# Ordering the chunks of a feed-forward block whose second product uses seven block products

## The chip, the cores and the metric

The kernel runs on one core of a Trainium2 chip. The metric is the device time of one execution in microseconds (us); less is better. A core has TensorE (PE: matmuls, and PEld: loads of the stationary operand), VectorE (DVE), ScalarE (ACT), GpSimd (POOL) and SyncE (SP), which here only starts transfers from memory. Each engine works through its own list of instructions in order, and waits where one of them needs what another engine or a transfer has not yet delivered.

## The reference

A decoder layer on `x` of 256 rows by 1024 columns in float32: a normalisation, a wide input projection, two attention mixers that are merged, an output projection with a residual, and then a feed-forward block and a last normalisation. The change touches the feed-forward block alone:

```python
h2 = rmsnorm(x, norm2_g[layer])
u = jax.nn.relu(h2 @ w_ff1[layer])          # 1024 -> 4096
x = x + (u * u) @ w_ff2[layer]              # 4096 -> 1024
...
return rmsnorm(x, norm_f_g)
```

## The kernel before, in words

**Chunks.** All weights stream through the core as a list of chunks, `CHUNKS` (line 23), each 128 partitions by 2048 float32 columns (1 MB) at most. The work on one chunk on TensorE is called its slot, and slots follow each other in the order of the list. The feed-forward block begins at chunk `C_FF` = 28 with 16 chunks `ff1` (each gives 256 of the 4096 hidden columns) and 16 chunks `ff2` (each takes 256 of them to all 1024 outputs). ff2 number i needs the activations of ff1 number i. In this text a chunk is named by its kind and number, such as ff2 0.

**Three matmuls for one.** The float32 product is made of three matmuls of a faster type (float32r): each operand is split into a high part (ScalarE copies it into that type: `whi`, `sh`, `ah`) and a low part (VectorE subtracts the high part from the original: `wlo`, `sl`, `al`). `mm3` (line 219) issues high x high, high x low and low x high. So for a chunk an engine each has a conversion to do, `split` (line 103), before TensorE can start.

**Seven products for eight.** An ff2 chunk is, with its activations, a product of 2 x 2 blocks: two halves of the hidden columns, two halves of the rows, two halves of the output columns. Done plainly this is eight block products of 512 columns, 24 matmuls. For the first `NSEVEN` = 11 ff2 chunks the kernel uses a scheme with seven block products, 21 matmuls, which accumulate over the chunks in seven PSUM banks (`P["1"]` to `P["7"]`). It needs sums of weight blocks (`w_sums`: tile `wt`, three subtractions and an addition in three instructions) and of activation blocks (`act_sums`: tile `aq`, four small instructions), and more splitting: three weight blocks are used as they are (`w_singles`: `sh`, `sl`), four are sums (`w_parts`: `whi`, `wlo`), and seven activation blocks (`act_parts`: `ah`, `al`). `combine` (line 880) puts the seven banks together into the residual `x1` at the end of these chunks. The other five ff2 chunks are done plainly and accumulate in four banks (`ops`).

**Order.** Nothing reorders the program: each engine's list is the order in which the code issues. `at(pos, f, ...)` notes a step, and `run_slot` (line 202) issues a slot's matmuls with each step put in at its share `pos` of the slot. So a step at 0.5 of a slot stands in its engine's list after the steps of 0.3, but it runs when its engine gets there and its inputs are ready. `slot_events(c)` (line 920) notes in slot c the conversions of chunk c+2 or c+3 and the load of chunk c+5.

**Buffers.** The raw weights, `whi` and `wlo` have three buffers each; a load waits on SyncE until the last conversion that reads the buffer's old content is done. `sh`, `sl`, `wt` and `aq` have two, `ah` and `al` three. Hidden columns of an ff1 chunk are summed in one PSUM bank (`acc0` from ff1 2 on) and leave it by a ReLU on ScalarE (`ur`), then a square (`aq`): `squares` (line 796).

**Order of chunks before.** ff1 0, then ff1 1, ff2 0, ff1 2, ff2 1, and so on to ff1 11, ff2 10; then the ff1 chunks 12 to 15 alone, then the plain ff2 chunks 11 to 15. In ff1 1's slot TensorE also transposes the residual into rows (`x1_rows`). The last two ff2 chunks, 14 and 15, form one last slot ordered by output bank, so that each bank's final work (`final_a`, `final_b`) can begin while the next is summed.

## Time and profile before

| | |
|---|---|
| three runs, median (lowest to highest) | 390.91 us (389.94 to 391.99) |
| profiled execution, whole time | 391.41 us |
| its span, first to last instruction | 389.5 us |
| first matmul of ff1 0, from the span's start | 199.80 us |
| last stage of matmuls ends | 383.43 us |
| mean granted TensorE clock | 0.988 |

The span begins with the first instruction and ends with the last; all places below are in us from its start. The feed-forward block is its second half. A row of a timeline gives start and duration, the engine, the line, the operation, output and inputs by the program's names, the shape, and in brackets the engine's idle time just before, with what ended it. The name `o` stands for the four banks o0 to o3.

### The profile page before, as it was taken

The numbers are of one execution on the slowest core, as the hardware profiler recorded it, in microseconds if no ns is written. First come the engines' busy times: TensorE is split into PE (matmuls) and PEld (weight loads), VectorE is DVE, ScalarE is ACT, GpSimd is POOL, SyncE is SP. The second block draws the span as 40 slices with busy tenths as digits, with TensorE's granted clock in tenths as the row PEclk, the third lists the DMA queues.
The fourth block names the chain that finished last, engine by engine and source line by source line (L and its number), as shares of the span: only waits on it lengthen the run. The fifth ranks groups of instructions, "written<-read, shape, count | busy, mean of one in ns | idle before, by whom it ended". The sixth has DMA issues, their size and how long they took to land.

```text
span 389.5 us, 5979 instructions
## 1 busy us (share of the span) xinstructions
PE 373.1 (96%) x2407; PEld 324.4 (83%) x2407; DVE 305.5 (78%) x443; ACT 231.4 (59%) x368; POOL 3.8 (1%) x14
## 2 busy tenths in 40 slices
PE   7999999999999999999998799999999999889993
PEld 6997888878888788779998599999998888888783
DVE  4968677887876869666969968999999999922565
ACT  6884455766755747444457567776666668451712
POOL 1000000000000000000000000000000000000001
PEclk9999999999999999999999699999999999999998
DMA  7977435233533334530846633566655556554003
GB/s 248 406 264 270 165 106 203 108 115 118 202 109 109 134 151 151 213 108 18 316 155 218 215 108 121 204 217 215 217 193 186 174 207 217 213 178 146 0 2 109
DMA packets 11260, 66.31 MB, mean 170 GB/s; under 512 B 1248, under 2 KB 2784, under 8 KB 3936
## 3 DMA queue, kind: packets, MB, share of 16 engines
q1 hardware_dynamic: 10800, 65.14, 46.8%
q10 hardware_dynamic: 432, 0.79, 0.5%
q8 instruction: 19, 0.31, 0.3%
q14 instruction: 9, 0.07, 0.0%
HBM read 64.87 MB, written 1.05 MB: 169 GB/s over the span
## 4 chain that ended last, share of the span: by engine, by line
PE 82%; DVE 8%; ACT 4%; issue 2%; DMA 1%; SPq 1%; POOLq 0%; POOL 0%; DVEq 0%; ACTq 0%
PE acc L217 51%; PE o L217 11%; PE yb L217 5%; PE tp L217 4%; DVE wlo L114 3%; PE kvbacc L217 2%; ACT whi L112 2%; PE qacc L217 2%; PE Sa L217 1%; DMA raw<-in_kva_dram 1%; PE Sb L217 1%; PE Sa L482 1%; PE Sb L482 1%; PE tp L298 1%; DVE wlo L862 1%
## 5 line engine op out<-in xcount | busy, mean ns | idle before, releaser
L114 DVE TENSOR_TENSOR wlo<-raw,whi 128x1024 fp32r<-128x1024 f32 (+3 forms) x87 | 114.5, 1333 | 28.9 <-ACT whi L112 28.8
L112 ACT ACTIVATE whi<-raw 128x1024 fp32r<-128x1024 f32 (+2 forms) x106 | 99.7, 975 | 46.9 <-PE acc L217 33.3
L217 PE MATMUL acc<-h2h,whi 128*128 128x256 f32 x240 | 66.8, 278 | 3.0 <-ACT ur L804 3.0
L217 PE MATMUL acc<-h2h,wlo 128*128 128x256 f32 x240 | 66.5, 277 | 0.0
L217 PE MATMUL acc<-h2l,whi 128*128 128x256 f32 x240 | 66.5, 277 | 0.0
L217 PE MATMUL acc<-whi,hTh 128*128 128x512 f32 (+1 forms) x128 | 50.8, 397 | 0.8 <-ACT whi L112 0.6
L217 PE MATMUL acc<-wlo,hTh 128*128 128x512 f32 (+1 forms) x128 | 50.6, 395 | 0.4 <-DVE wlo L114 0.2
L217 PE MATMUL acc<-whi,hTl 128*128 128x512 f32 (+1 forms) x128 | 49.4, 386 | 0.0
L217 PEld LDWEIGHTS acc<-h2h,whi 128*128 128x128 f32 x240 | 45.1, 188 | 3.9 <-ACT ur L804 3.4
L217 PEld LDWEIGHTS acc<-h2l,whi 128*128 128x128 f32 x240 | 45.1, 188 | 0.5
L217 PEld LDWEIGHTS acc<-h2h,wlo 128*128 128x128 f32 x240 | 45.1, 188 | 0.0
L860 ACT ACTIVATE whi<-wt 128x2048 fp32r<-128x2048 f32 x11 | 21.1, 1920 | 24.7 <-DVE wt L845 24.7
L217 PEld LDWEIGHTS acc<-whi,hTh 128*128 128x128 f32 x128 | 24.2, 189 | 6.8 <-ACT whi L112 1.1
L217 PEld LDWEIGHTS acc<-wlo,hTh 128*128 128x128 f32 x128 | 24.1, 188 | 5.5 <-DVE wlo L114 1.6
L217 PEld LDWEIGHTS acc<-whi,hTl 128*128 128x128 f32 x128 | 24.1, 188 | 4.3
L862 DVE TENSOR_TENSOR wlo<-wt,whi 128x2048 fp32r<-128x2048 f32 x11 | 25.1, 2286 | 0.4 <-ACT whi L860 0.4
L820 ACT ACTIVATE ah<-aq 128x896 fp32r<-128x896 f32 (+1 forms) x16 | 13.6, 852 | 18.1 <-PE o L217 10.0
L822 DVE TENSOR_TENSOR al<-aq,ah 128x896 fp32r<-128x896 f32 (+1 forms) x16 | 15.4, 960 | 6.7 <-ACT ah L820 6.7
L853 DVE TENSOR_TENSOR sl<-raw,sh 128x1536 fp32r<-128x1536 f32 x11 | 19.3, 1752 | 0.0
L217 PE MATMUL o<-wlo,ah 128*128 128x512 f32 (+1 forms) x47 | 18.9, 402 | 0.0
L217 PE MATMUL o<-whi,al 128*128 128x512 f32 (+1 forms) x47 | 18.8, 400 | 0.0
L217 PE MATMUL o<-whi,ah 128*128 128x512 f32 (+1 forms) x47 | 18.8, 400 | 0.0
(280 smaller groups left out, 759.5 us busy)
## 6 DMA issues: line engine op xcount, KB each, us to landing
raw<-in_ff_dram SPq DMA_DIRECT2D x32, 1024.0 KB, 4.8
raw<-in_gm_dram SPq DMA_DIRECT2D x8, 1024.0 KB, 4.8
raw<-in_wout_dram SPq DMA_DIRECT2D x4, 1024.0 KB, 4.8
raw<-in_q_dram SPq DMA_DIRECT2D x2, 1024.0 KB, 5.5
raw<-in_qm_dram SPq DMA_DIRECT2D x2, 1024.0 KB, 7.6
raw<-in_km_dram SPq DMA_DIRECT2D x2, 1024.0 KB, 5.8
raw<-in_vm_dram SPq DMA_DIRECT2D x2, 1024.0 KB, 4.8
raw<-in_upn_dram SPq DMA_DIRECT2D x2, 1024.0 KB, 4.8
```

The costliest lines, as they stand in the source:

```text
L112: act.activation(hi[c][:, a:b], raw[c][:, a:b], AF.Copy)
L114: dve.tensor_tensor(lo[c][:, a:b], raw[c][:, a:b], hi[c][:, a:b].bitcast(F32), op=ALU.subtract)
L217: pe.matmul(o, l, r, start=start, stop=stop, skip_group_check=True)
L298: pe.transpose(tp[:, j * 256 + t * 128:j * 256 + t * 128 + 128], src[:, t, (2 * i + j) * 128:(2 * i + j + 1) * 128], ident)
L482: pe.transpose(S[x][:, j, c:c + 128], P[:, 2 * x + j, c:c + 128], ident)
L820: act.activation(A[i][1][:, 0:b - a], aq[:, a:b], AF.Copy)
L822: dve.tensor_tensor(A[i][2][:, 0:b - a], aq[:, a:b], A[i][1][:, 0:b - a].bitcast(F32), op=ALU.subtract)
L853: dve.tensor_tensor(singles[c][1], v, singles[c][0].bitcast(F32), op=ALU.subtract)
L860: act.activation(hi[c], v, AF.Copy)
L862: dve.tensor_tensor(lo[c], v, hi[c].bitcast(F32), op=ALU.subtract)
```

## The change

The list of chunks begins with three ff1 chunks; then ff2 and ff1 chunks come in turns until the ff1 chunks are used up (ff2 0, ff1 3, ff2 1, ... ff2 12, ff1 15), and ff2 13, 14 and 15 stand at the end. `NSEVEN` is 13, so all ff2 chunks that stand in turns use seven products and three are plain. The sums of weights and of activations of a chunk become one step, `sums`, in which an instruction of one kind stands between two of the other. The steps move within the slots: the sums and the high singles of an ff2 chunk are issued in the ff1 slot three chunks ahead, the rest of its conversions in the ff2 slot two chunks ahead, its activations' parts too. `ah` and `al` have two buffers for three. The combining stands in the slots of ff1 15 and ff2 13.

```diff
-NSEVEN = 11
+NSEVEN = 13
...
-    + [("ff1", 0, 2048)]
-    + [(s, i + (s == "ff1"), 2048) for i in range(NSEVEN) for s in ("ff1", "ff2")]
-    + [("ff1", i, 2048) for i in range(NSEVEN + 1, 16)]
+    + [("ff1", i, 2048) for i in range(3)]
+    + [(s, i + 3 * (s == "ff1"), 2048) for i in range(NSEVEN) for s in ("ff2", "ff1")]
     + [("ff2", i, 2048) for i in range(NSEVEN, 16)]
...
-    def act_sums(i):
-        aq = A[i][0]
-        if i < NSEVEN:
-            for o, x, y, op in ((4, 0, 2, ALU.add), (5, 1, 0, ALU.subtract),
-                                (6, 4, 1, ALU.subtract), (7, 3, 6, ALU.subtract)):
-                dve.tensor_tensor(aq[:, o], aq[:, x], aq[:, y], op=op)
...
-            A[i] += [FB["p"].tile([128, 7, 128], F32R, name=n, bufs=3) for n in ("ah", "al")]
+            A[i] += [FB["p"].tile([128, 7, 128], F32R, name=n, bufs=2) for n in ("ah", "al")]
...
-    def w_sums(c):
+    def sums(c):
...
+        aq = A[CHUNKS[c][1]][0]
+
+        def a_sum(o, x, y, op):
+            dve.tensor_tensor(aq[:, o], aq[:, x], aq[:, y], op=op)
+
         dve.tensor_tensor(T[:, 0:2], b[:, 1:4:2], b[:, 0, None, :].to_broadcast([128, 2, 512]),
                           op=ALU.subtract)
+        a_sum(4, 0, 2, ALU.add)
+        a_sum(5, 1, 0, ALU.subtract)
         dve.tensor_tensor(T[:, 2], b[:, 3], T[:, 0], op=ALU.add)
+        a_sum(6, 4, 1, ALU.subtract)
         dve.tensor_tensor(T[:, 3], b[:, 2], T[:, 2], op=ALU.subtract)
+        a_sum(7, 3, 6, ALU.subtract)
...
+        if seven(c + 2):
+            if c + 2 == C_FF + 3:
+                at(0.1, w_singles, c + 2, "h")
+                at(0.12, sums, c + 2)
+            at(0.15, w_parts, c + 2, "h")
+            at(0.2, w_singles, c + 2, "l")
+            at(0.3, load, c + 5)
+            at(0.35, w_parts, c + 2, "l")
+            if c + 2 > C_FF + 3:
+                at(0.4, act_parts, CHUNKS[c + 2][1], "h")
+                at(0.6, act_parts, CHUNKS[c + 2][1], "l")
+        elif c + 2 < NCH:
+            if c == C_FF + 2:
+                at(0.03, act_parts, 0, "h")
+                at(0.05, act_parts, 0, "l")
+            if seven(c + 3) and c >= C_FF + 2:
+                at(0.05, sums, c + 3)
+                at(0.5, w_singles, c + 3, "h")
             for k in range(2):
-                at(0.3 * k, split, c + 2, k, 2, "h")
+                at(0.04 + 0.3 * k, split, c + 2, k, 2, "h")
             at(0.46, split, c + 2, 0, 1, "l")
             at(0.51, load, c + 5)
...
+        i = {NCH - 6: 13, NCH - 5: 14}.get(c, 0)
+        if i:
+            at(0.55, act_parts, i, "h")
+            at(0.65, act_parts, i, "l")
...
-            if i == NSEVEN + 1:
-                at(0.1, combine, 0)
-                at(0.35, combine, 1)
-                at(0.7, combine, 2)
+            if i == 15:
+                at(0.3, combine, 0)
+                at(0.7, combine, 1)
...
             if i == 1:
-                at(0.9, rstd2)
+                at(0.7, rstd2)
...
             if i == NSEVEN:
-                ops.update({order[0]: P["4"], order[1]: o_bank(0), order[2]: P["2"],
+                ops.update({order[0]: P["4"], order[1]: bank("acc0", "acc"), order[2]: P["2"],
                             order[3]: P["3"]})
+                at(0.2, combine, 2)
+                at(0.3, act_parts, 15, "h")
+                at(0.4, act_parts, 15, "l")
```

Three places show what this does to the engines' lists. The first is VectorE from ff1 1's split on, that is, ahead of the first seven-product chunk, ff2 0. Before (`wlo<-raw` of 1024 columns twice is ff1 1's split, L842 to L845 the sums of weights, L813 those of activations):

```order
L114 TENSOR_TENSOR wlo<-raw,whi 128x1024 x2
L842 TENSOR_TENSOR wt<-raw 128x1024
L844 TENSOR_TENSOR wt<-raw,wt 128x512
L845 TENSOR_TENSOR wt<-raw,wt 128x512
L853 TENSOR_TENSOR sl<-raw,sh 128x1536
L862 TENSOR_TENSOR wlo<-wt,whi 128x2048
L813 TENSOR_TENSOR aq<-aq 128x128 x4
L114 TENSOR_TENSOR wlo<-raw,whi 128x2048
```

The same place of the changed kernel (its line numbers differ: L113 is the split, L840 to L846 the weights' sums, L838 the activations', L814 `al`):

```order
L113 TENSOR_TENSOR wlo<-raw,whi 128x1024 x2
L113 TENSOR_TENSOR wlo<-raw,whi 128x2048
L840 TENSOR_TENSOR wt<-raw 128x1024
L838 TENSOR_TENSOR aq<-aq 128x128 x2
L844 TENSOR_TENSOR wt<-raw,wt 128x512
L838 TENSOR_TENSOR aq<-aq 128x128
L846 TENSOR_TENSOR wt<-raw,wt 128x512
L838 TENSOR_TENSOR aq<-aq 128x128
L855 TENSOR_TENSOR sl<-raw,sh 128x1536
L864 TENSOR_TENSOR wlo<-wt,whi 128x2048
L814 TENSOR_TENSOR al<-aq,ah 128x896
```

The split of the third ff1 chunk moved ahead of all of ff2 0's work, and `al` follows at once.

The second place is VectorE in one pair of chunks of the middle. Before, from the split of an ff1 chunk on:

```order
L114 TENSOR_TENSOR wlo<-raw,whi 128x2048
L842 TENSOR_TENSOR wt<-raw 128x1024
L844 TENSOR_TENSOR wt<-raw,wt 128x512
L845 TENSOR_TENSOR wt<-raw,wt 128x512
L853 TENSOR_TENSOR sl<-raw,sh 128x1536
L813 TENSOR_TENSOR aq<-aq 128x128 x4
L862 TENSOR_TENSOR wlo<-wt,whi 128x2048
L822 TENSOR_TENSOR al<-aq,ah 128x896
```

Of the changed kernel, from the sums of an ff2 chunk on:

```order
L840 TENSOR_TENSOR wt<-raw 128x1024
L838 TENSOR_TENSOR aq<-aq 128x128 x2
L844 TENSOR_TENSOR wt<-raw,wt 128x512
L838 TENSOR_TENSOR aq<-aq 128x128
L846 TENSOR_TENSOR wt<-raw,wt 128x512
L838 TENSOR_TENSOR aq<-aq 128x128
L113 TENSOR_TENSOR wlo<-raw,whi 128x2048
L855 TENSOR_TENSOR sl<-raw,sh 128x1536
L864 TENSOR_TENSOR wlo<-wt,whi 128x2048
L814 TENSOR_TENSOR al<-aq,ah 128x896
```

The same instructions stand in both; the sums moved ahead of the split and are interleaved, and the split stands between the sums and the low singles, so the two instructions that free a raw buffer, L113 and L855, are neighbours.

The third place is the end of ScalarE's list before the first evictions of the output. Before (L820 is `ah`, its last row that of ff2 15; the four halves behind it are `whi` of the last two chunks):

```order
L804 ACTIVATE ur<-o_3445 128x512
L805 ACTIVATE aq<-ur 128x512
L112 ACTIVATE whi<-raw 128x1024
L820 ACTIVATE ah<-aq 128x512
L112 ACTIVATE whi<-raw 128x1024 x4
```

Of the changed kernel (L812 is `ah`):

```order
L803 ACTIVATE ur<-acc 128x512
L804 ACTIVATE aq<-ur 128x512
L111 ACTIVATE whi<-raw 128x1024
L812 ACTIVATE ah<-aq 128x512
L111 ACTIVATE whi<-raw 128x1024
```

One half of `whi`, that of ff2 15, is left behind the last `ah`.

## The prediction

> **What bounds the kernel now.** I first read the page's head for the engines' shares.

> ```profile
> span 389.5 us, 5979 instructions
> ...
> PE 373.1 (96%) x2407; PEld 324.4 (83%) x2407; DVE 305.5 (78%) x443; ACT 231.4 (59%) x368; POOL 3.8 (1%) x14
> ```

> TensorE is busy 96% of the span, so time can come from two places only: fewer or faster matmuls, or its few gaps. The change leaves everything ahead of the first ff1 chunk alone, so I cut the rest, from that chunk's first matmul at 199.80, at the stage borders, and read busy time per stage (columns: stretch, its length, busy PE, PEld, DVE, ACT, POOL, granted clock, DMA share, GB/s).

> ```profile
> core 0: us, PE busy (x) PEld busy (x) DVE busy (x) ACT busy (x) POOL busy (x), PEclk, DMA share, GB/s
> 199.80:217.50 17.70, 13.64 (x117) 13.01 (x115) 16.35 (x19) 12.61 (x17) 0.00 (x0) 0.97 0.51 168
> 217.50:224.67 7.17, 7.17 (x19) 5.65 (x20) 5.71 (x7) 2.41 (x2) 0.00 (x0) 0.59 0.50 179
> 224.67:276.28 51.61, 51.61 (x346) 47.06 (x345) 47.22 (x51) 35.88 (x37) 0.00 (x0) 1.00 0.49 172
> 286.62:329.02 42.40, 42.38 (x277) 37.38 (x276) 41.44 (x43) 30.11 (x30) 0.00 (x0) 1.00 0.56 199
> 329.02:354.82 25.80, 22.77 (x193) 22.36 (x192) 16.81 (x16) 12.91 (x17) 0.00 (x0) 1.00 0.52 193
> 354.82:372.00 17.18, 17.11 (x74) 13.49 (x73) 7.03 (x5) 8.08 (x10) 0.00 (x0) 1.00 0.19 61
> 372.00:383.43 11.43, 11.43 (x61) 9.55 (x59) 7.76 (x15) 3.06 (x9) 0.56 (x1) 1.00 0.14 48
> 383.43:389.50 6.07, 0.00 (x1) 0.00 (x0) 1.90 (x7) 1.15 (x5) 0.55 (x1) 0.81 0.25 87
> ```

> Five stages lose time. Before the first seven-product chunk TensorE stands 4 us. After it the clock is 0.59. The five pairs from 224.67 take 51.61/5 = 10.32 us each, the four from 286.62 take 42.40/4 = 10.60 with VectorE busy 41.44 of 42.40. The four lone ff1 chunks from 329.02 take 25.80. The next rows show the first loss on TensorE (start, duration, what was waited for).

> ```profile
> 212.42 0.28 PE L217 MATMUL acc<-h2h,wlo 128*128 128x256 f32 x1
> 214.60 0.50 PE L217 MATMUL o<-sh,ah 128*128 128x512 f32 x1 [1.90 <-ACT x L761]
> ...
> 217.49 0.79 PE L217 MATMUL o<-sh,al 128*128 128x512 f32 x1 [2.16 <-DVE al L822]
> ```

> ff2 0's weights and activations are not split when TensorE arrives. The price of one pair stands in the chain of work that ended last:

> ```profile
> 230.29 2.79 PE o L217 x12
> 233.08 0.68 PE yb L217 x3
> 233.76 0.68 PE acc L217 x3
> 234.44 0.70 PE tp L217 x3
> 235.14 5.48 PE acc L217 x48
> ```

> So a seven-product chunk is 2.79+0.68+0.68+0.70 = 4.85 (21 matmuls of 0.23), an ff1 chunk 5.48, a pair 10.33; a plain ff2 chunk of 24 matmuls is 24 x 0.2335 = 5.6.

> **The change on TensorE.** ff1 0 starts at 199.80 as before. ff1 1, with the x1 transposes inside it, ends at 212.42+0.12 = 212.54. Then ff1 2 follows, which was behind ff2 0: 5.47, so ff2 0 starts at 218.0. Then 13 pairs: 13 x 10.33 = 134.3, to 352.3. The plain ff2 13: to 357.9. The last stretch 11.43 and the tail 6.07 (both rows above) are the same work: 375.4, if TensorE never waits. The rest is whether it waits.

> **Start.** Durations and places of before:

> ```profile
> 203.67 1.22 DVE L842 TENSOR_TENSOR wt<-raw 128x1024 f32<-128x1024 f32 x1
> ...
> 209.90 0.64 ACT L805 ACTIVATE aq<-ur 128x512 f32<-128x512 f32 x1
> ...
> 211.74 0.95 ACT L820 ACTIVATE ah<-aq 128x896 fp32r<-128x896 f32 x1 [0.26 <-DVE aq L813]
> ```

> VectorE is free at 203.67, and has ff1 2's split and all of ff2 0's work ahead: by the next fence one pair's work, 10.3, so it is done by 214.0 without waits. The last wait is ScalarE's: the `ah` of ff2 0 is now queued behind ReLU and square of ff1 1, which start at 212.5: 0.64+0.64+0.95 (the ReLU taken like the square), 214.9 with some overlap, then `al` 1.1: 216.0. Its first use is 218.0. So the stall goes, with 2 us to spare. Without a stall I expect no clock of 0.59. Before, 7.17 went on 19 matmuls that cost 4.4 otherwise.

> **A pair on VectorE.** One pair of before (start, duration), and the group of the four small sums:

> ```profile
> 239.60 2.29 DVE L114 TENSOR_TENSOR wlo<-raw,whi 128x2048 fp32r<-128x2048 f32 x1 [1.53 <-ACT whi L112]
> 241.81 1.22 DVE L842 TENSOR_TENSOR wt<-raw 128x1024 f32<-128x1024 f32 x1
> 243.06 0.69 DVE L844 TENSOR_TENSOR wt<-raw,wt 128x512 f32<-128x512 f32 x1
> 243.79 0.69 DVE L845 TENSOR_TENSOR wt<-raw,wt 128x512 f32<-128x512 f32 x1
> 244.40 1.75 DVE L853 TENSOR_TENSOR sl<-raw,sh 128x1536 fp32r<-128x1536 f32 x1
> 246.07 1.02 DVE L813 TENSOR_TENSOR aq<-aq 128x128 f32<-128x128 f32 x4
> 247.00 2.28 DVE L862 TENSOR_TENSOR wlo<-wt,whi 128x2048 fp32r<-128x2048 f32 x1
> 249.20 1.08 DVE L822 TENSOR_TENSOR al<-aq,ah 128x896 fp32r<-128x896 f32 x1
> 250.21 2.29 DVE L114 TENSOR_TENSOR wlo<-raw,whi 128x2048 fp32r<-128x2048 f32 x1
> ...
> L813 DVE TENSOR_TENSOR aq<-aq 128x128 f32<-128x128 f32 x4 | 1.0, 288 | 0.0
> ```

> From split to split 10.61, all busy. L844 needs L842's result and starts 0.03 after its end (243.06 against 241.81+1.22). L853 needs nothing of L845 and starts 0.08 before its end. A direct dependence thus costs 0.11. There are three: L842 to L844, L844 to L845, and one among the four small sums (4 x 0.288 = 1.15 last 1.02, that is two overlaps of 0.08 and one gap of 0.03). Interleaved, each result has another instruction behind it before it is read: 10.60 - 3 x 0.11 = **10.27**. In parts: sums 3.19, split 2.20, singles' low 1.67, sums' low 2.20, `al` 1.01. The bounds are 10.60 (no gain) and 10.27; I take 10.27, since both kinds of neighbours stand in these rows. Then TensorE's 10.33 is the longer.

> [...]

> **A new circle through the load.** In the new order the three-buffer raw tile of an ff1 chunk is freed by its split, the load issued then brings the ff2 chunk whose sums stand three VectorE instructions later. Loads in four windows (225 to 360; issued at 188; at 190; at 273), with size and us from issue to landing:

> ```profile
> raw<-in_ff_dram SPq DMA_DIRECT2D x24, 1024.0 KB, 4.8
> ...
> raw<-in_ff_dram SPq DMA_DIRECT2D x1, 1024.0 KB, 6.0
> ...
> raw<-in_ff_dram SPq DMA_DIRECT2D x1, 1024.0 KB, 7.1
> ...
> raw<-in_ff_dram SPq DMA_DIRECT2D x1, 1024.0 KB, 6.1
> ```

> The circle is sums 3.19 + split 2.20, to its end 0.09, load 4.8, and some 0.05 at both ends: **10.33**. That ties with TensorE. Behind waiting sums stand the next split and all of the pair, so a longer load delays all of it. TensorE has something in hand: from `al` at 216.0 on, sums to 219.2, ff1 3's split to 221.4, due at 222.85; one pair later, with the load landing at 226.3, to 231.7 against 233.2, less the two 128x2 instructions of rstd2, each below the 0.29 of a 128x128 one. So about 1.2 us is spare there, and the seven-product chunks have 2. Loads of 4.9 cost nothing over eleven pairs; a single 6.1 takes 1.3. I add 0.3 for this. Bounds: 4.8 and 7.1 for the load, that is 0 and some 26 us; I stay near 4.8, which is the middle of 24.

> The second load of a pair is now issued one instruction after the first (1.7) and overlaps it; before, the tiles came free 4.2 apart (239.60+2.29 and 244.40+1.75). Its chunk is wanted only some 12 us after its issue.

> **End.** The lone ff1 chunks' waits go (25.80 - 4 x 5.47 = 3.9), because a seven-product chunk now stands between one bank's use and the next. The combining moves into ff1 15 and ff2 13, where VectorE has no sums: six of 0.7 to 0.75, hidden; with no cover they would cost 4.5. New is a wait: `ah` and `al` have two buffers for three. The last `ah`, of ff2 15, must wait until ff2 13 has read its own, at the end of that chunk. Rows for durations:

> ```profile
> 360.46 0.63 ACT L820 ACTIVATE ah<-aq 128x512 fp32r<-128x512 f32 x1 [8.05 <-PE o L217]
> 361.00 1.05 ACT L112 ACTIVATE whi<-raw 128x1024 fp32r<-128x1024 f32 x1
> ...
> 361.13 0.69 DVE L822 TENSOR_TENSOR al<-aq,ah 128x512 fp32r<-128x512 f32 x1 [6.39 <-ACT ah L820]
> ...
> 368.65 2.29 DVE L114 TENSOR_TENSOR wlo<-raw,whi 128x2048 fp32r<-128x2048 f32 x1 [1.21 <-ACT whi L112]
> ```

> Queued behind it on ScalarE is the second half of ff2 15's `whi`, and behind that on VectorE its `wlo`: 357.9, `ah` 0.54 to the next, `whi` 1.05 to 359.5, `wlo` 2.29 to 361.8. TensorE wants that `wlo` at its eighth matmul of the last stretch, 357.9 + 7 x 0.2335 = 359.5. So it stands **2.4 us**. Nothing hides this: each bank of the last stretch needs ff2 15, and the order of matmuls is fixed.

> **Sum.** 375.4 + 2.4 = 377.8 of span, +0.3 for loads. Check from the other side: start 4.5, clock 2.7, four pairs 4 x 0.27 = 1.1, lone chunks 3.9, 355 to 372 0.35, six matmuls 1.4 make 13.9; less 2.4 is 11.5, and 389.5 - 11.5 = 378.0. The profiled execution took 391.41 for a span of 389.54, so 1.9 lies around it: 380.0. It was 0.5 above the median of the three runs, 390.91; for the median I say **379.4**.

> **Rivals.**
> - Interleaving saves nothing (10.60 a pair): twelve pairs lose 0.27 each, 3.2, of which 1.2 is covered: 381.4. For it: the saving is read from neighbours of two sizes only; against: the overlaps in the rows. 0.08. [...]
> - The wait at the end brings the slow clock again. The first loss had 1.90 and 2.16 with two matmuls between, and 0.59 after; waits of 1.5 in the lone chunks had 1.00. A single 2.4 lies between. Half the rate for some 7 us costs up to 3.4: 382.8. 0.10.
> - The overlap stretches a pair's first load halfway from 4.8 to the 6.0 of the load at 188, to 5.4: the circle is 10.93, 0.6 x 12 - 1.2 = 6: 385.4. For it: the loads of 6.0 and 7.1 had others within 2.2 us of them; against: there the 512 KB load of gfb was on its way too, and the lone load at 273 took 6.1, so a long load needs no neighbour. 0.13.
> - Slower: the same place at its worst. TensorE gains some 11.5 and has 1.2 spare, over 12 pairs 1.06 each, so from a load of 5.9 on the change loses. At 6.0 the circle is 11.53: 1.2 x 12 - 1.2 = 13.2, 392.6; at 7.1 it would be 405. 0.06.
> - No stall at the end: 377.0. For it, nothing that I see but a mistake in my order of the last waits. 0.03.

> The forecast, 378.5 to 381, has 0.60. The range 377 to 385 holds it, the first two rivals, the last, and the milder part of the third: 0.81 and a little. A measurement of this kernel tells about 0.5% from no change, 2 us: faster 0.93, same 0.01, slower 0.06.

> [...]

> **What will show it.** No PE wait above 0.5 us between 205 and 345 and PEclk at 1.00 there; ff2 0's first product near 218.0; pairs at 10.33; neighbours in the sums overlapping by 0.08; no VectorE wait on raw over 0.3 on average; one PE wait of 2.4 on `wlo` near 359. Wrong would be: the first load of a pair landing after 5 us or more, or a VectorE pair above 10.4.

## The result, and the profile after

| | before | changed |
|---|---|---|
| median of four runs each | 391.25 us | 381.90 us |
| lowest to highest | 389.94 to 391.99 | 381.59 to 382.16 |
| profiled execution, whole time | 391.41 us | 381.83 us |
| its span | 389.5 us | 380.1 us |
| mean granted TensorE clock | 0.988 | 0.992 |

The changed kernel takes 0.9764 of the time before [0.9736, 0.9793], some 9.3 us less. The forecast was 379.4, so 2.5 us too low. All below is read against the sum of the prediction: 377.8 of span and 0.3 for loads.

First the head of the page of the changed kernel.

```profile
span 380.1 us, 5982 instructions
...
PE 368.2 (97%) x2401; PEld 322.7 (85%) x2401; DVE 312.8 (82%) x459; ACT 235.6 (62%) x368; POOL 3.8 (1%) x14
```

TensorE has 6 matmuls less (2407 before). VectorE is busy 7.3 us longer than before, though it became no bound; two more chunks have sums to make. Next the stages of the changed kernel, cut where the prediction cuts them: ff1 0 to 2, the 13 pairs, ff2 13, the last stage, the tail. Columns as before.

```profile
core 0: us, PE busy (x) PEld busy (x) DVE busy (x) ACT busy (x) POOL busy (x), PEclk, DMA share, GB/s
200.00:218.40 18.40, 18.40 (x162) 18.40 (x161) 15.78 (x20) 14.36 (x18) 0.00 (x0) 1.00 0.46 173
218.40:352.70 134.30, 134.30 (x900) 122.46 (x899) 130.72 (x138) 95.42 (x96) 0.00 (x0) 1.00 0.53 196
352.70:358.30 5.60, 5.60 (x27) 4.51 (x25) 3.93 (x6) 2.18 (x3) 0.00 (x0) 1.00 0.00 0
358.30:373.70 15.40, 13.21 (x61) 10.62 (x59) 9.59 (x16) 4.64 (x11) 0.56 (x1) 0.89 0.10 35
373.70:380.10 6.40, 0.00 (x0) 0.00 (x0) 1.89 (x7) 1.16 (x5) 0.55 (x1) 0.78 0.23 83
```

For 158 us, from 200.0 to 358.3, TensorE's busy time equals the stretch and its clock is 1.00. The 13 pairs last 134.30, against 134.3 in the sum. What is lost lies in the fourth row: 15.40 for the 61 matmuls that took 11.43 before. It holds 2.2 us in which TensorE stands, and a clock of 0.89.

The rows of one pair on VectorE, from the sums of an ff2 chunk to those of the next (L838 are the activations' sums, L840, L844 and L846 the weights', L113 the split):

```profile
216.11 1.22 DVE L840 TENSOR_TENSOR wt<-raw 128x1024 f32<-128x1024 f32 x1
217.25 0.49 DVE L838 TENSOR_TENSOR aq<-aq 128x128 f32<-128x128 f32 x2
217.65 0.69 DVE L844 TENSOR_TENSOR wt<-raw,wt 128x512 f32<-128x512 f32 x1
218.25 0.29 DVE L838 TENSOR_TENSOR aq<-aq 128x128 f32<-128x128 f32 x1
218.46 0.69 DVE L846 TENSOR_TENSOR wt<-raw,wt 128x512 f32<-128x512 f32 x1
219.06 0.29 DVE L838 TENSOR_TENSOR aq<-aq 128x128 f32<-128x128 f32 x1
219.26 2.29 DVE L113 TENSOR_TENSOR wlo<-raw,whi 128x2048 fp32r<-128x2048 f32 x1
221.46 1.76 DVE L855 TENSOR_TENSOR sl<-raw,sh 128x1536 fp32r<-128x1536 f32 x1
...
226.43 1.22 DVE L840 TENSOR_TENSOR wt<-raw 128x1024 f32<-128x1024 f32 x1
```

Every sum starts about 0.08 before the record of the one ahead of it ends (217.25 against 216.11 + 1.22 = 217.33). The sums take 219.26 - 216.11 = 3.15, the whole pair 10.32. At the pair's end stands the load: the transfer that the split of 219.26 lets go lands, by the trace, at 226.41, and the next sums start at 226.43. By the trace, eight of the eleven later sums start 0.02 to 0.03 after such a landing. So the circle through the load and TensorE's pair are a tie, as worked out. From the list of waits after 199 us:

```profile
ACT ah L812 <- PE acc L216: 3.2, 1, 3.2
...
PEld tp L216 <- DVE wlo L113: 2.6, 1, 2.6
...
PE tp L216 <- DVE wlo L113: 2.2, 1, 2.2
...
DVE wt L840 <- DMA raw<-in_ff_dram: 1.8, 3, 1.3
```

VectorE waited for a load three times in 13 pairs, 1.8 us in all, and none of this reached TensorE. TensorE waited once, for a `wlo`. The rows around that wait, first of ScalarE and VectorE, then of TensorE (L812 is `ah`, L111 a half of `whi`):

```profile
358.33 0.63 ACT L812 ACTIVATE ah<-aq 128x512 fp32r<-128x512 f32 x1 [3.23 <-PE acc L216]
358.86 1.05 ACT L111 ACTIVATE whi<-raw 128x1024 fp32r<-128x1024 f32 x1
...
359.94 2.29 DVE L113 TENSOR_TENSOR wlo<-raw,whi 128x2048 fp32r<-128x2048 f32 x1 [0.26 <-ACT whi L111]
...
359.71 0.39 PE L216 MATMUL tp<-whi,ah 128*128 128x512 f32 x1
362.29 0.50 PE L216 MATMUL tp<-wlo,ah 128*128 128x512 f32 x1 [2.19 <-DVE wlo L113]
...
363.88 0.63 PE L216 MATMUL acc<-wlo,ah 128*128 128x512 f32 x1
364.31 0.63 PE L216 MATMUL acc<-whi,al 128*128 128x512 f32 x1
```

`ah` waits 3.23 for ff2 13's last product on `acc`, which frees its buffer. Behind it stand the half of `whi` and then `wlo`, and TensorE goes on 2.58 after the matmul ahead, 2.35 more than its usual 0.23. From 363.7 the matmuls then follow at 0.43 instead of 0.23: half the clock (granted 0.50), until 367.1. That is eight matmuls at 0.2 too much each, 1.6 us.

### The profile page after: what moved, and what is told of

It is laid out like the page before. It is cut to its first block, busy times and chain, and to the rows that moved or that the text cites. A ratio compares the mean times of both kernels' runs of the same rounds, so it can differ in the third digit from the quotient of the medians.

```text
span 380.1 us, 5982 instructions
## 1 busy us (share of the span) xinstructions
PE 368.2 (97%) x2401; PEld 322.7 (85%) x2401; DVE 312.8 (82%) x459; ACT 235.6 (62%) x368; POOL 3.8 (1%) x14
## 3 DMA queue, kind: packets, MB, share of 16 engines
HBM read 64.87 MB, written 1.05 MB: 173 GB/s over the span
## 4 chain that ended last, share of the span: by engine, by line
PE 89%; DVE 3%; ACT 2%; issue 2%; DMA 1%; SPq 1%; POOLq 0%; POOL 0%; DVEq 0%; ACTq 0%
PE acc L216 58%; PE o L216 10%; PE yb L216 5%; PE tp L216 4%; PE qacc L216 3%; PE kvbacc L216 2%; DVE wlo L113 2%; DMA raw<-in_kva_dram 1%; PE Sa L216 1%; ACT whi L111 1%; PE Sb L216 1%; PE Sb L481 1%; PE Sa L481 1%; PE tp L297 1%; DVE hTl L172 0%
## 5 line engine op out<-in xcount | busy, mean ns | idle before, releaser
L113 DVE TENSOR_TENSOR wlo<-raw,whi 128x1024 fp32r<-128x1024 f32 (+3 forms) x85 | 109.9, 1311 | 13.0 <-ACT whi L111 13.0
L111 ACT ACTIVATE whi<-raw 128x1024 fp32r<-128x1024 f32 (+2 forms) x102 | 95.5, 973 | 38.6 <-PE acc L216 23.1
L216 PE MATMUL acc<-h2h,whi 128*128 128x256 f32 x256 | 71.0, 277 | 0.0
L216 PE MATMUL acc<-h2h,wlo 128*128 128x256 f32 x256 | 71.0, 277 | 0.0
L216 PE MATMUL acc<-h2l,whi 128*128 128x256 f32 x256 | 70.9, 277 | 0.0
L864 DVE TENSOR_TENSOR wlo<-wt,whi 128x2048 fp32r<-128x2048 f32 x13 | 29.7, 2288 | 0.1
L853 ACT ACTIVATE sh<-raw 128x1536 fp32r<-128x1536 f32 x13 | 19.4, 1489 | 16.0 <-DMA raw<-in_ff_dram 16.0
L862 ACT ACTIVATE whi<-wt 128x2048 fp32r<-128x2048 f32 x13 | 24.8, 1908 | 2.5 <-DVE wt L846 2.5
L855 DVE TENSOR_TENSOR sl<-raw,sh 128x1536 fp32r<-128x1536 f32 x13 | 22.8, 1754 | 0.0
L814 DVE TENSOR_TENSOR al<-aq,ah 128x896 fp32r<-128x896 f32 (+1 forms) x16 | 16.2, 1013 | 4.0 <-ACT ah L812 4.0
L216 PE MATMUL acc<-mxl,whi 128*128 128x256 f32 x64 | 17.8, 278 | 0.2 <-DVE mxl L669 0.2
L216 PE MATMUL acc<-mxh,wlo 128*128 128x256 f32 x64 | 17.9, 279 | 0.0
L216 PE MATMUL acc<-mxh,whi 128*128 128x256 f32 x64 | 17.7, 276 | 0.0
## 6 DMA issues: line engine op xcount, KB each, us to landing
raw<-in_ff_dram SPq DMA_DIRECT2D x32, 1024.0 KB, 5.6
raw<-in_gm_dram SPq DMA_DIRECT2D x8, 1024.0 KB, 4.7
raw<-in_wout_dram SPq DMA_DIRECT2D x4, 1024.0 KB, 4.8
raw<-in_q_dram SPq DMA_DIRECT2D x2, 1024.0 KB, 7.2
raw<-in_qm_dram SPq DMA_DIRECT2D x2, 1024.0 KB, 7.0
raw<-in_km_dram SPq DMA_DIRECT2D x2, 1024.0 KB, 5.0
raw<-in_vm_dram SPq DMA_DIRECT2D x2, 1024.0 KB, 4.7
raw<-in_upn_dram SPq DMA_DIRECT2D x2, 1024.0 KB, 4.7
```

The source lines that it names most:

```text
L111: act.activation(hi[c][:, a:b], raw[c][:, a:b], AF.Copy)
L113: dve.tensor_tensor(lo[c][:, a:b], raw[c][:, a:b], hi[c][:, a:b].bitcast(F32), op=ALU.subtract)
L216: pe.matmul(o, l, r, start=start, stop=stop, skip_group_check=True)
L814: dve.tensor_tensor(A[i][2][:, 0:b - a], aq[:, a:b], A[i][1][:, 0:b - a].bitcast(F32), op=ALU.subtract)
L853: act.activation(singles[c][0], v, AF.Copy)
L855: dve.tensor_tensor(singles[c][1], v, singles[c][0].bitcast(F32), op=ALU.subtract)
```

## The experiments

The medians of the kernel before on the same chips were 390.83 (11 runs, beside `k1` to `k4`) and 391.02 (7 runs, beside `k5`, `k6` and `k8`). Ratios are against these.

**1. The wait at the end, taken away by a third buffer** (`k1_three_buffers`).

```diff
-            A[i] += [FB["p"].tile([128, 7, 128], F32R, name=n, bufs=2) for n in ("ah", "al")]
+            A[i] += [FB["p"].tile([128, 7, 128], F32R, name=n, bufs=3) for n in ("ah", "al")]
```

> The changed kernel with three buffers for ah and al again, as before the change. My theory: the last ah no longer waits for the end of ff2 13, so the wlo of ff2 15 is ready by 359.6, TensorE's wait of 2.35 us goes, and with it the stretch of clock 0.5 behind it (1.6 us): 381.9 - 4.0 = about 378.0. Rival A (the wait comes from the amount of work on VectorE at the end, not from the buffer): a wait of 1.5 or more stays, time 380.5 to 382. Rival B (the slow clock at the end has nothing to do with the wait): the wait goes, the slow stretch stays, 379.5.

Measured: 377.81 (377.37 to 379.03), ratio 0.9675 [0.9656, 0.9694]. That is 4.1 below the changed kernel. ScalarE's rows at the same place, and the stretch from ff2 13 to the last matmul:

```profile
354.67 1.04 ACT L111 ACTIVATE whi<-raw 128x1024 fp32r<-128x1024 f32 x1
355.62 0.62 ACT L812 ACTIVATE ah<-aq 128x512 fp32r<-128x512 f32 x1
356.14 1.05 ACT L111 ACTIVATE whi<-raw 128x1024 fp32r<-128x1024 f32 x1
...
353.30:370.33 17.03, 17.03 (x86) 14.08 (x84) 13.02 (x22) 6.71 (x14) 0.56 (x1) 1.00 0.09 32
370.33:376.40 6.07, 0.00 (x0) 0.00 (x0) 1.89 (x7) 1.16 (x5) 0.55 (x1) 0.85 0.25 86
```

`ah` follows `whi` at once. The stretch takes 17.03 with TensorE always busy at full clock; in the changed kernel it takes 5.60 + 15.40 = 21.00. The difference, 3.97, is the wait of 2.35 and the 1.6 of slow clock. So the lost time is this wait with what it brings.

**2. The same wait left, what is queued behind it moved ahead** (`k2_wlo_first`). Two buffers stay; ff2 15's `ah` and `al` are issued later in ff2 13's slot, so that both halves of its `whi` and its `wlo` stand ahead of them.

```diff
-                at(0.3, act_parts, 15, "h")
-                at(0.4, act_parts, 15, "l")
+                at(0.4, act_parts, 15, "h")
+                at(0.5, act_parts, 15, "l")
```

> The changed kernel with two buffers, but with both halves of ff2 15's whi and its wlo issued ahead of the last ah and al. My theory: what costs is the queue behind the waiting ah, not the wait itself; ah is ready at 359.0 and first wanted at 359.7, al at 359.7 and first wanted at 360.2, so TensorE does not wait: about 378.0, as with three buffers. Rival (the late activations themselves hold TensorE): it still waits 0.5 to 2 us for ah or al, 379 to 381.5.

Measured: 378.26 (377.62 to 379.10), ratio 0.9683 [0.9666, 0.97]. The rows show why:

```profile
357.17 2.28 DVE L113 TENSOR_TENSOR wlo<-raw,whi 128x2048 fp32r<-128x2048 f32 x1
...
358.85 0.64 ACT L812 ACTIVATE ah<-aq 128x512 fp32r<-128x512 f32 x1 [2.28 <-PE acc L216]
```

`ah` still waits, 2.28, to the end of ff2 13. But `wlo` ran already at 357.17, and TensorE does not stand there. The time was the queue's, not the buffer's: here the wait cost what stood behind it in its engine's list. TensorE has one wait left in this trace, 0.49 at 316.87 for a `wlo` of the pairs, after a load that took 6.5.

**3. The sums not interleaved** (`k3_sums_apart`). The three sums of weights come first, the four of activations after them; all else as changed.

```diff
         dve.tensor_tensor(T[:, 0:2], ...)
+        dve.tensor_tensor(T[:, 2], b[:, 3], T[:, 0], op=ALU.add)
+        dve.tensor_tensor(T[:, 3], b[:, 2], T[:, 2], op=ALU.subtract)
         a_sum(4, 0, 2, ALU.add)
         a_sum(5, 1, 0, ALU.subtract)
-        dve.tensor_tensor(T[:, 2], b[:, 3], T[:, 0], op=ALU.add)
         a_sum(6, 4, 1, ALU.subtract)
-        dve.tensor_tensor(T[:, 3], b[:, 2], T[:, 2], op=ALU.subtract)
         a_sum(7, 3, 6, ALU.subtract)
```

> The changed kernel with the seven sums not interleaved: the three of the weights first, then the four of the activations, everything else the same. My theory: three direct dependences come back, each 0.11 us, so VectorE's pair goes from 10.27 to 10.60 against TensorE's 10.33; 12 pairs lose 0.27, and of the 1.9 us that VectorE is ahead at first a part is used up by loads already: 2 to 3 us slower, about 384.4, TensorE's waits spread over the last pairs. Rival (the next instruction never starts before the pipe is empty, whatever it needs): no change, 381.9, neighbours at the same distances.

Measured: 387.06 (385.23 to 388.55, six runs), ratio 0.9905 [0.9881, 0.9929]. The direction is as expected, the size is not: 5.2 above the changed kernel, where 2.5 was expected. VectorE's rows of a pair, and one of TensorE's later gaps:

```profile
228.12 1.22 DVE L840 TENSOR_TENSOR wt<-raw 128x1024 f32<-128x1024 f32 x1
229.37 0.69 DVE L842 TENSOR_TENSOR wt<-raw,wt 128x512 f32<-128x512 f32 x1
230.10 0.69 DVE L843 TENSOR_TENSOR wt<-raw,wt 128x512 f32<-128x512 f32 x1
230.71 1.01 DVE L838 TENSOR_TENSOR aq<-aq 128x128 f32<-128x128 f32 x4
231.64 2.28 DVE L113 TENSOR_TENSOR wlo<-raw,whi 128x2048 fp32r<-128x2048 f32 x1
...
293.44 1.23 DVE L840 TENSOR_TENSOR wt<-raw 128x1024 f32<-128x1024 f32 x1 [1.02 <-DMA raw<-in_ff_dram]
...
299.31 0.38 PE L216 MATMUL acc<-h2h,wlo 128*128 128x256 f32 x1 [1.11 <-DVE wlo L113]
```

A sum that reads the one ahead starts 0.03 after its end (229.37 against 229.34), and the sums take 3.52 instead of 3.15. But the sums also lie on the circle through the load, which becomes 3.52 + 2.20 + 0.09 + 4.8 + 0.05 = 10.66 against TensorE's 10.33. By the prediction's spare of 1.2 us, that is used up after four pairs. From then on a longer load has no cover: the load issued at 287.57 takes 5.8, VectorE waits 1.02 at 293.44, and TensorE stands at 299.31. The 13 pairs take 138.9.

**4. The same, with a fourth buffer for raw weights** (`k6_sums_apart_4_raw`). It takes the load out of the circle and leaves the sums apart, which tells the two reasons of the last run from each other.

```diff
-        raw[c] = wp.tile([128, 2048], F32, name="raw")
+        if c > C_FF + 5 and c % 4 == 0:
+            raw[c] = FB["p"].tile([128, 2048], F32, name="raw4")
+        else:
+            raw[c] = wp.tile([128, 2048], F32, name="raw")
```

> The kernel with the sums not interleaved, with a fourth buffer for raw weights from chunk 36 on, so that a load no longer waits for the split of the same pair. My theory: of the 5.2 us that taking the sums apart cost, only VectorE's own 0.27 a pair stays (12 x 0.27 - 1.9 = 1.3); the rest was the circle through the load, since the longer sums stand in it: about 383.3. Rival (VectorE itself loses more than 0.33 a pair when the sums stand apart): 386 to 387 as with three buffers.

Measured: 383.00 (382.25 to 383.37), ratio 0.9796 [0.978, 0.9811]. In the list of waits VectorE's wait on raw weights is gone. Its pairs now run at its own pace, 10.59 from sums to sums:

```profile
321.91 1.22 DVE L843 TENSOR_TENSOR wt<-raw 128x1024 f32<-128x1024 f32 x1
...
332.50 1.22 DVE L843 TENSOR_TENSOR wt<-raw 128x1024 f32<-128x1024 f32 x1
```

So of the 5.2 us that the interleaving is worth in this kernel, 1.1 remain by the medians when loads come early enough: that is VectorE's own part. In the profiled executions it is somewhat more: the 13 pairs take 136.2 here, 138.9 with three raw buffers and 134.3 with the sums interleaved, so 1.9 of 4.6 remain. The rest, 3 to 4 us, is the circle, which the interleaving shortens too. The changed kernel with the fourth raw buffer alone was not run; where the end is free, that buffer changes little (experiments 2 and 7).

**5. The start alone** (`k4_start_alone`). The code before, with its steps at their old places in the slots as far as they still fit, and three ff1 chunks ahead: eleven seven-product chunks, sums apart, three buffers of `ah` and `al`, two lone ff1 chunks instead of four.

```diff
-    + [("ff1", 0, 2048)]
-    + [(s, i + (s == "ff1"), 2048) for i in range(NSEVEN) for s in ("ff1", "ff2")]
-    + [("ff1", i, 2048) for i in range(NSEVEN + 1, 16)]
+    + [("ff1", i, 2048) for i in range(3)]
+    + [(s, i + 3 * (s == "ff1"), 2048) for i in range(NSEVEN) for s in ("ff2", "ff1")]
+    + [("ff1", i, 2048) for i in range(NSEVEN + 3, 16)]
```

> The kernel before with the order of chunks of the change and nothing else: three ff1 chunks ahead, then in turns, 11 chunks with seven products, sums not interleaved, two ff1 chunks alone ahead of the plain ff2 chunks. My theory: the 4.5 us wait before ff2 0 and the 2.7 us lost to the slow clock behind it go, and about half of the waits of the lone ff1 chunks; VectorE's pair of 10.60 takes some back: 391.25 - 7.2 - 1.6 + 0 to 1.5 = 382.5 to 384. Rival (the gain came from the two chunks more and the interleaving): 388 to 391.

Measured: 383.49 (383.04 to 383.60), ratio 0.9813 [0.9799, 0.9828], within what was expected. The start has no wait and no slow clock, as the first row of its stages shows; then the pairs fall to VectorE's pace (10.60 from sums to sums by the trace), and a lone chunk waits:

```profile
200.00:218.30 18.30, 18.30 (x162) 18.30 (x161) 16.93 (x21) 15.10 (x19) 0.00 (x0) 1.00 0.45 174
...
PEld o L217 <- DVE wlo L862: 2.9, 7, 0.4
...
335.33 0.38 PE L217 MATMUL acc<-h2h,whi 128*128 128x256 f32 x1 [1.52 <-ACT ur L804]
```

By the trace ff1 3 begins at 223.14 in this kernel, when three ff1 chunks and ff2 0 are done; before, the same work was done at 224.67 + 5.48 = 230.15. So the order at the start is worth 7.0 us, without interleaving and without more seven-product chunks, and it carries most of the change. The rest of this kernel's order nearly cancels: the lone chunks wait once and not four times, and more pairs run at 10.60.

**6. Longer loads** (`k5_longer_loads`). The rival that ends slower says that the changed kernel loses its gain when the first load of a pair lands after 5.9 us. Here the loads of eleven ff2 chunks are split into a first sixteenth and the rest, and a transfer of 512 KB that nothing reads is put between the two.

```diff
+            if c > C_FF + 5 and CHUNKS[c][0] == "ff2" and CHUNKS[c][1] < NSEVEN:
+                load_part(c, 0, 16)
+                spare = FB["p"].tile([128, 1024], F32, name="spare")
+                nc.sync.dma_start(spare, w["ff2"][0, :, 0:1024])
+                load_part(c, 1, 16, 15)
+                return
             load_part(c, 0, 1)
```

> The changed kernel with a 512 KB transfer into a spare tile put into the middle of eleven of the ff2 loads, so that these loads land later. My theory: sums, split and load form a circle, so a pair takes 5.5 us plus the time from the load's first issue to its landing; at some 6.5 us that is 12.0 instead of 10.33, and eleven pairs lose 1.67 each less 1.9 that VectorE is ahead: about 398 (395 to 402). Rival (loads are hidden, the sums wait for VectorE's turn): no change, 381.9 to 383.

Measured: 410.49 (410.22 to 411.83), ratio 1.0499 [1.0482, 1.0517]. The loads came out longer than meant, 7.0 to 9.0 and 7.5 in the mean from the first issue to landing, so the time expected is too low. With this length the circle is 5.5 + 7.5 = 13.0 a pair; ten pairs from 221.2 on took 131.2, 13.1 each. One wait of VectorE, its sum over all of them, and the stretch of ten pairs:

```profile
241.08 1.23 DVE L846 TENSOR_TENSOR wt<-raw 128x1024 f32<-128x1024 f32 x1 [2.09 <-DMA raw<-in_ff_dram]
...
DVE wt L846 <- DMA raw<-in_ff_dram: 30.0, 11, 4.2
...
221.20:352.40 131.20, 114.34 (x700) 102.54 (x699) 103.43 (x114) 75.67 (x76) 0.00 (x0) 0.93 0.55 201
```

The DMA share of that row, 0.55, is hardly above the 0.53 of the changed kernel's pairs, so the amount of data alone does not explain the longer pairs. The mechanism of that rival is real, and the kernel is then slower than before by 5%. Only, in the changed kernel's trace a single load of a pair's sums got that long.

**7. Both remedies** (`k8_wlo_first_4_raw`): experiment 2 with the fourth raw buffer of experiment 4, whose diffs it joins.

> The changed kernel with ff2 15's wlo ahead of the last ah, and the fourth raw buffer. My theory: without the circle a long load costs nothing, so the waits that loads left (0.5 us in the profile with wlo first) go: 377.8, with runs closer together. Rival (the fourth buffer brings loads that collide with others): 378.5 or more.

Measured: 378.04 (377.75 to 379.12), ratio 0.9676 [0.9658, 0.9695]. Experiments 1, 2 and 7 can't be told apart. With the sums interleaved and the end free, the loads cost nothing that the medians show. The third buffer of `ah` and `al`, an edit of one digit, is the simplest version that beats both kernels, by 3.2% and, by the medians, 1.1%.

## Why the prediction was off by 2.5 us, point by point

- **What bounds it.** TensorE, without a gap from 200 to 358: right, and the measured time lies in the range of 377 to 385, though above the narrower forecast of 378.5 to 381. The gain is gaps, clock and six matmuls.
- **The change on TensorE, and the start.** ff2 0 was to start at 218.0 without a wait. Its first product came at 218.42 by the trace; half of the 0.4 was there already at ff1 0 (200.03 against 199.80). `k4_start_alone` shows the start by itself: 7.0 us, against 4.5 for the stall and 2.7 for the clock.
- **A pair on VectorE.** Overlap of 0.08 between independent neighbours, a gap of 0.03 between dependent ones: both seen, in the changed kernel and in `k3_sums_apart`. Three times 0.11 was the forecast, 3.52 - 3.15 = 0.37 was measured. VectorE's own work in a pair is 3.15 + 2.20 + 1.67 + 2.20 + 1.01 = 10.23, where 10.27 was forecast. The rival in which interleaving saves nothing fell: with loads out of the way it saves 1.1 us by the medians (383.00 for `k6_sums_apart_4_raw`, 381.90 for the changed kernel).
- **A new circle through the load.** 10.33 was the sum; 10.32 is what the row of one pair shows, the landing ending it. The two rivals in which the overlapped loads stretch the circle (385.4 and 392.6) fell: a pair's first load took 4.7 to 5.2 in the trace but for one of 6.1, which the spare time took up. The second load, issued 1.7 later, took 5.5 to 7.2 and was wanted only afterwards. The 0.3 added for loads was not needed. But the lead was nearly used up. From 216.11 to 331.32 eleven pairs of VectorE took 115.21, where TensorE's take 113.6, so 1.6 of a lead that the prediction put at 1.2 to 2 went, most of it on waits for loads. At 10.47 a pair, VectorE even passed the 10.4 that the prediction had named as a sign of being wrong, and no gap came of it. How near the edge this is, `k3_sums_apart` and `k5_longer_loads` show.
- **End.** A wait of 2.4 at the last stage's eighth matmul, from `ah` by way of `whi` and `wlo`: right in place and cause, and 2.35 at that matmul. The prediction's own terms make 2.25 (0.54 + 1.05 + 2.29 less 7 x 0.2335), so part of the exact number is luck. Experiments 1 and 2 show the links through the buffer and the queue.
- **The step that failed** stands among the rivals: "The wait at the end brings the slow clock again", at 0.10, with the reason that the waits known to slow the clock had come in a pair and "a single 2.4 lies between" them and the harmless 1.5. It came, and cost 1.6, not the 3.4 at most. The sum so put the slow clock at nothing, and the eight matmuls behind the wait paid. The mistake was to judge by the length of single waits: the 1.90 and 2.16 before the change lay so close together that TensorE was busy for only 0.73 of the 3.41 us from 213.12, so they could not tell what one wait does. What the rows show of it stands in the last section.
- **Sum.** 377.8 + 0.4 at the start + 1.6 of clock + 0.3 in the tail (6.40 against 6.07) = 380.1, the span. The tail's 0.3 lies behind the issue of the last output transfer, from which it is 3.9 to the end (376.16 to 380.05) where the kernel before and `k1_three_buffers` have 3.65; what made it longer is open. The span is thus 2.0 above the forecast's 377.8 + 0.3. The other 0.5 is the step from the span to the median. The prediction took off about 0.5 because the profiled run before had been that much above its median; this time the two are equal (381.83 and 381.90).
- **Not tried.** The two further seven-product chunks by themselves: 1.4 by the count of matmuls, which the page confirms (2401 for 2407) and no run times alone.

## What to carry to other kernels

When a buffer is taken away, price the new wait by what is queued behind the waiting instruction on its engine: moving two steps by a tenth of a slot did as much here as giving the buffer back (378.26 and 377.81). Where a load is released by the work that a pair of chunks does, write the circle down (work up to the release, load, first use) and keep it below the bound engine's time, with room for the longest load in the trace; an edit that shortens the work on such a circle can be worth several times what it saves on the engine's own list (here 5.2 us against 1.1 to 1.9). And charge a wait of 2 us on TensorE with the slow clock that may follow: here the 2.35 brought 1.6 us of it, though in `k5_longer_loads` a wait of 2.12 had a clock of 1.00 behind it.

## What the runs showed of the clock

```profile
213.12:216.53 3.41, 0.73 (x2) 0.30 (x2) 3.34 (x5) 3.38 (x7) 0.00 (x0) 1.00 0.50 115
216.54:219.95 3.41, 2.46 (x6) 1.98 (x7) 3.38 (x6) 2.42 (x2) 0.00 (x0) 0.50 0.46 192
...
360.26:363.67 3.41, 1.38 (x6) 1.16 (x7) 2.37 (x2) 0.00 (x0) 0.00 (x0) 1.00 0.00 0
363.68:367.09 3.41, 3.41 (x10) 2.66 (x9) 1.59 (x3) 0.72 (x2) 0.00 (x0) 0.50 0.00 0
...
310.79:314.20 3.41, 1.62 (x14) 1.63 (x15) 3.41 (x3) 3.41 (x4) 0.00 (x0) 1.00 0.11 29
314.21:317.62 3.41, 3.41 (x33) 3.41 (x32) 3.18 (x2) 0.59 (x1) 0.00 (x0) 1.00 0.94 311
...
361.99:365.40 3.41, 1.53 (x9) 1.19 (x8) 3.41 (x4) 2.98 (x4) 0.00 (x0) 1.00 0.00 0
365.41:368.82 3.41, 3.41 (x18) 3.41 (x17) 3.41 (x3) 2.29 (x3) 0.00 (x0) 0.50 0.77 281
```

Behind the stretches busy for 0.73, 1.38 or 1.53 of 3.41 the clock is 0.50; behind the one busy for 1.62 it is 1.00. The length of a wait does not tell these rows apart: by its trace `k5_longer_loads` has a wait of 2.12 around the line at 310.79, which cuts it in two, with a clock of 1.00 behind it, and one of 1.88 wholly inside the stretch from 361.99, with 0.50 behind it. In the traces of the kernel before and of the changed kernel each fall has such a stretch ahead of it, busy for 0.73 and 1.38, and for 0.00 in the two tails; every other stretch from the trace's first record of the clock to its last fall is busy for 2.07 or more. One fall is not like these: by its trace `k3_sums_apart` has a stretch from 6.39 busy for 1.78, more than the 1.62, that was followed by half the clock. So the busy time of one stretch goes with the slow clock in these rows, but it does not tell all, and no run was made to try it.

The grid's lines lie at another place in each of these two executions: counted back from the changes, one falls on the first record of the clock, at 4.90 in the trace of the kernel before and at 5.28 in that of the changed kernel. That a wait of 2.4 can be cut in two by a line and pass, as the 2.12 did, is my estimate and was not shown. All four runs of the changed kernel had a mean clock of 0.990 to 0.992, where three of the four of `k1_three_buffers` had 0.997 or 0.998, so the slow stretch probably fell into each of them; that the others were not profiled leaves this open.
